# A third seven-product pair in the FFN's first product, with four smaller edits to the order of work

## The chip, the cores and the metric

The kernel runs on one core of one Trainium2 chip. The metric is the device time of one execution in microseconds (us); the time of a version is the median of its runs. TensorE (PE in the profile) multiplies, VectorE (DVE) and ScalarE (ACT) do everything elementwise, GpSimd (POOL) does almost nothing here, and SyncE (SP) issues the loads. Each engine runs its own instructions in the order in which the program lists them.

## The reference, cut to what matters

The program is a two-layer decoder trunk on 256 rows of width 2048, in float32. Each layer adds a token mixer (layer 0: pooling; layer 1: sparse attention with rotary tables), a cross attention to a memory, and a SwiGLU feed-forward block (FFN). The change is almost wholly inside the FFN:

```
FFN_HIDDEN = 5632
def swiglu(h, w_in, w_out):
    g, u = jnp.split(h @ w_in, 2, axis=-1)
    return (jax.nn.silu(g) * u) @ w_out

for i in range(2):
    ...
    x = x + swiglu(rms_norm(x, norm_ffn[i]), ffn_w_in[i], ffn_w_out[i])
```

## The kernel before

**Numbers in two halves.** Every float32 weight is split into a high part (the rounded value) and a low part (the rest), and a product is three matmuls: high times high, high times low, low times high. A weight *piece* is one load of 128 x 2048 numbers (1 MB) into one of 3 `raw` buffers. ACT makes the high part (`high`, L167) and DVE the low part (`low`, L170). Split pieces live in 8 `w` buffers of 128 x 2048.

**The FFN.** The first product is done in 11 chunks of 512 hidden columns (`chunk_in(j)`, j = 0 to 10); each needs 512 gate and 512 up columns and all 2048 input rows, that is 8 pieces or *pairs* (256 input rows each, `kp` = 0 to 7). The second product (`chunk_out`) runs after chunks 4, 8 and 10, twice each, on the hidden rows made so far. Both use `blocks`, which has four accumulators, one for each output half f (0: gate, 1: up) and each half t of the 256 rows. A *plain* pair has four *slots* of 6 matmuls, one for each accumulator; a slot is followed by `hook()`. A *seven* pair does the same 2 x 2 x 2 block product with seven products in place of eight (a Strassen form), 21 matmuls in place of 24. It needs sums of weight blocks, which DVE makes in place (L204, L207, L208), four `w` buffers (bh, bl, th, tl) in place of two, and sums of the operand (`combine`). The products that several outputs share gather in four more PSUM banks (the `sm` and `tp` ones). When the last seven pair of a chunk has ended, `mid` (L849) works these up: one ACT copy and four DVE operations.

**The end of a chunk.** The last pair is plain. After each of its slots `done(f, t)` (L864) issues a DVE addition (L867) that empties this accumulator, for f = 0 also the silu on ACT, for f = 1 a DVE multiply. The next chunk takes the four accumulator banks again. In the compiled program of the kernel before, an accumulator gets its bank at its first matmul, and takes the one that came free longest ago: the k-th slot of a new chunk waits for the k-th addition of the chunk before, whichever accumulators these are.

**What sets the order on DVE and ACT.** `hook()` (L277) runs at most one waiting job, then `split_unit()` (L227) once, or twice if the next piece is not yet split. One call issues the ACT part of the next splitting step and then the DVE part of the step *before* (`owed`): the stagger. A plain piece has two steps, a seven piece four (`d0` to `d3`). `split_seven` (L188) begins with `d0`: two lows and the 1024-wide sum L204, then `d1`: L207 and L208. A step that needs `w` buffers is only begun if no more than `cap` = 8 of them are held, by the piece in use (a seven pair gives two back after its third product, L823) and those ahead of it. So the splitting runs at most some three pieces ahead, and where it stops depends on where the seven pairs stand. `seven()` issues any job still waiting before the first seven pair of a chunk (L806).

**Other places touched.** `combine` (L415) uses `sums` buffers. `Normed.chunk` (L484) makes, beside the transposed operand, a scaled copy (`scaled`, L409) for each pair in `SEVEN`. In layer 0, `tables()` (L957) makes the rotary tables for layer 1's attention; its two functions are queued as jobs, with a delay of 6 hooks, before the last two `chunk_out` calls. The first products of the program (memory keys, pieces `xk`) stand at L609.

Of the kernel before, what the change touches and what calls it, by code (L numbers as in the profile page):

```python
# [13 lines left out]
F32R = mybir.dt.float32r  # L14
# [6 lines left out]
P = 128  # L21
# [8 lines left out]
FH = 5632  # L30
HT = FH // 512

SEVEN = (3, 5)


SEVEN_OUT = (3, 5, 11, 13, 18)
PAIRS_FIRST, SEVEN_FIRST, PAIRS = (0, 1, 2, 4, 3, 5, 6, 7), (3,), tuple(range(8))
EPS = 1e-6
TOPK = 64
KVI = 336  # L40
# [18 lines left out]
W_SHORT = 6  # L59
# [5 lines left out]
def trunk_kernel(ctx: ExitStack, tc: tile.TileContext, a: dict, out: bass.AP):  # L65
# [70 lines left out]
                for kp in range(2 * t0, 2 * t1):  # L136
                    plan(("fo", L, n, kp), a["fo"][L, n, kp], kp in SEVEN_OUT)

    state = {"load": 0, "split": 0, "cur": 0, "hook": 0, "held": 0, "cap": W_SHORT, "begun": 0}
    raws, parts, steps, owed = {}, {}, deque(), deque()  # L140
    UNIT = 1024

# [23 lines left out]
    def high(dst, src):  # L166
        A.activation(dst, src, AF.Copy)  # L167

    def low(dst, src, hi):
        V.tensor_tensor(dst, src, hi.bitcast(F32), op=ALU.subtract)  # L170
# [17 lines left out]
    def split_seven(i, t):  # L188

        r = t.rearrange("p (s c) -> p s c", s=4)  # L190
        p = {}
        own, outer = (slice(0, 1024), slice(1536, 2048)), (slice(1536, 2048), slice(0, 512))

        def a0():
            p["bh"], p["bl"] = w_tile("bh"), w_tile("bl")
            parts[i] = p
            for c in own:
                high(p["bh"][:, c], t[:, c])

        def d0():  # L200

            for c in own:
                low(p["bl"][:, c], t[:, c], p["bh"][:, c])
            V.tensor_tensor(r[:, 1:3, :], r[:, 1:4:2, :], r[:, 2:3, :].to_broadcast([P, 2, 512]), op=ALU.add)  # L204

        def d1():
            V.tensor_tensor(r[:, 3, :], r[:, 1, :], r[:, 3, :], op=ALU.add)  # L207
            V.tensor_tensor(r[:, 0, :], r[:, 3, :], r[:, 0, :], op=ALU.add)  # L208

        def a2():  # L210
            p["th"], p["tl"] = w_tile("th"), w_tile("tl")
            high(p["th"][:, 512:1536], t[:, 512:1536])

        def d2():
            low(p["tl"][:, 512:1536], t[:, 512:1536], p["th"][:, 512:1536])

        def a3():
            for c in outer:
                high(p["th"][:, c], t[:, c])

        def d3():
            for c in outer:
                low(p["tl"][:, c], t[:, c], p["th"][:, c])

        return [(2, a0, d0), (0, None, d1), (2, a2, d2), (0, a3, d3)]

    def split_unit(must=False):  # L227

        i = state["begun"]
        if not steps and i < len(pieces):  # L230
            load_to(i + 1)
            new = split_seven(i, raws[i][0]) if pieces[i][2] else split_plain(i, *raws[i])
            steps.extend((n, act, dve, i if j == len(new) - 1 else None) for j, (n, act, dve) in enumerate(new))
            state["begun"] += 1
        dve = end = None
        if steps and state["held"] + steps[0][0] <= (W_BUFS if must else state["cap"]):
            _, act, dve, end = steps.popleft()
            if act is not None:
                act()
        assert owed or dve is not None or not must  # L240
        if owed:
            fn, of = owed.popleft()
            fn()
            if of is not None:
                raws.pop(of)
                state["split"] += 1
                load_to(of + 1 + RAW_BUFS)
        if dve is not None:
            owed.append((dve, end))

    def w_get(key, ahead=0):
        i = state["cur"] + ahead
# [161 lines left out]

    def combine(f):  # L415

        s = work.tile([P, 1024], F32R, tag="sums", name="sums", bufs=4)
        c = tmp()
        a11, a21, a12, a22 = (f[:, i * P:(i + 1) * P] for i in range(4))
        s4, s2, s1, s3 = (c[:, i * P:(i + 1) * P] for i in range(4))  # L420
        V.tensor_tensor(s1, a21, a22, op=ALU.subtract)
        V.tensor_tensor(s3, a11, a21, op=ALU.subtract)
        V.tensor_tensor(s2, s1, a11, op=ALU.subtract)
        V.tensor_tensor(s4, s2, a12, op=ALU.add)
        high(s[:, 0:512], c)
        return s, lambda: low(s[:, 512:1024], c, s[:, 0:512])
# [182 lines left out]
    for j in range(4):  # L609
        wh, wl = w_get(("xk", 0, j))  # L610
        xt = ms_get(j)
        for k in range(4):
            for h in range(XH):
                mm_T(k_acc[h], wh, wl, k * 512 + h * P, xt, k, j == k == 0, j == k == 3)
            if k < 3:
                hook()
        if j == 0:
            load_x()
        if j == 2:
            load_rest()  # L620
        w_done()
        hook()

# [146 lines left out]
    def ffn(L, xn, nxt, between=()):  # L770
        hs = {}

        sums = {}
# [8 lines left out]
        def blocks(keys, operand, mid, done, t_major=0):  # L782


            acc = [acc_tile() for _ in range(4)]
            m = {}
            seven_at = [i for i in range(len(keys)) if pieces[state["cur"] + i][2]]

            def plain(i, w, f, t):
                xt, k0, _ = operand(i)  # L790
                for u in range(2):
                    ws = c(((1, 2), (0, 3))[u][f])
                    three(acc[2 * t + f], xt[:, k0 + u, t * P:(t + 1) * P], xt[:, k0 + u, S + t * P:S + (t + 1) * P],
                          w[0][:, ws], w[1][:, ws], i == 0 and u == 0, i == len(keys) - 1 and u == 1)
                if i == len(keys) - 1:
                    done(f, t, acc[2 * t + f])

            def eight(i, w):
                for f, t in ((0, 0), (0, 1), (1, 0), (1, 1)):
                    plain(i, w, f, t)  # L800
                    if (f, t) != (1, 1):
                        hook()

            def seven(i, w):
                if not m:
                    while jobs:  # L806
                        run_job()
                    m.update({1: sm_tile(), 5: sm_tile(), 6: tp_tile(), 7: tp_tile()})
                xt, k0, s = operand(i)
                first, last = i == seven_at[0], i == seven_at[-1]  # L810

                def a_(t, u):
                    return xt[:, k0 + u, t * P:(t + 1) * P], xt[:, k0 + u, S + t * P:S + (t + 1) * P]

                def s_(j):
                    return s[:, j * P:(j + 1) * P], s[:, 512 + j * P:512 + (j + 1) * P]

                bh, bl, th, tl = (w[n] for n in ("bh", "bl", "th", "tl"))
                three(acc[1], *s_(0), bh[:, c(3)], bl[:, c(3)], False, False)
                three(acc[0], *a_(0, 1), bh[:, c(0)], bl[:, c(0)], False, False)  # L820
                hook()
                three(m[1], *a_(0, 0), bh[:, c(1)], bl[:, c(1)], first, last)
                state["held"] -= W_TILES  # L823
                three(acc[2], *a_(1, 1), th[:, c(0)], tl[:, c(0)], False, False)
                hook()
                for j, (p, si) in enumerate(((5, 2), (7, 3), (6, 1))):
                    three(m[p], *s_(si), th[:, c(j + 1)], tl[:, c(j + 1)], first, last)
                    if j == 1:
                        hook()
                if last:  # L830
                    mid(m)

            n = len(keys) - t_major
            for i in range(n):
                (seven if i in seven_at else eight)(i, w_get(keys[i]))
                if i < len(keys) - 1:
                    w_done()
                    hook()
            for t in range(2 if t_major else 0):
                for i in range(n, len(keys)):  # L840
                    w = w_get(keys[i], i - n)
                    for f in range(2):
                        plain(i, w, f, t)
# [62 lines left out]
        def chunk_out(n, t0, t1, last):  # L906
# [4 lines left out]
            def mid(m):  # L911
                v, u = tmp(), tmp()
                A.activation(v, m[1], AF.Copy)
                V.tensor_tensor(u, m[6], v, op=ALU.add)
                V.tensor_tensor(xc(0, 0), xc(0, 0), v, op=ALU.add)
                for f in range(2):
                    V.tensor_tensor(xc(1, f), m[5], xc(1, f), op=ALU.add)
                    V.tensor_tensor(xc(1, f), xc(1, f), u, op=ALU.subtract)
                    if f == 0:
                        V.tensor_tensor(u, m[7], u, op=ALU.add)  # L920
                V.tensor_tensor(xc(0, 1), xc(0, 1), u, op=ALU.add)

            def operand(i):
                kp = 2 * t0 + i
# [18 lines left out]
        for gi, (t0, t1) in enumerate(GROUPS):  # L943
            last = gi == len(GROUPS) - 1
            state["cap"] = W_BUFS
            for j in range(t0 + (gi > 0), t1 + (not last)):
                chunk_in(j)
            for fn in between if last else ():
                job(fn, 6)
            for n in range(2):  # L950
                chunk_out(n, t0, t1, last)
        state["cap"] = W_SHORT
# [345 lines left out]
```

## Time and profile before

| | us |
|---|---|
| median of 3 runs (1969.64 to 1970.30) | 1970.25 |
| the profiled execution, its own time | 1970.56 |
| span of the profiled execution, first to last instruction | 1968.8 |
| PE busy | 1946.9 |
| DVE busy | 1554.8 |
| ACT busy | 1026.8 |

Times in the profile are counted from the span's start. A busy time counts overlapping instructions of an engine once. Matmuls overlap: one is listed with some 0.39 us, but they start some 0.23 us apart, and two independent DVE operations also start a little less than one duration apart.

### The profile page before, as it was taken

Reading aid. Unit: us, or ns where it says so; the run is one execution under the profiler, and the core shown is the slowest. Engines: PE = TensorE matmul, PEld = TensorE weight load, DVE = VectorE, ACT = ScalarE, POOL = GpSimd, SP = SyncE. Lnnn points to the kernel's source line nnn. Section 1 sums busy time; section 2 is a strip of 40 time slices with the busy share of each in tenths; the row PEclk is TensorE's granted clock in tenths of the full one; section 3 lists DMA queues with packets and bytes.
Section 4 is the critical chain, followed back from the end, with each engine's and each line's share of the span. In section 5 each row is a group of like instructions: output and inputs, shape, how many; then the busy total and the mean of one; then the engine's idle time right before and its main releaser. Section 6 shows DMA issues by size and latency. Waiting matters only on the chain.

```text
span 1968.8 us, 23586 instructions
## 1 busy us (share of the span) xinstructions
PE 1946.9 (99%) x8986; PEld 1617.6 (82%) x8986; DVE 1554.8 (79%) x2229; ACT 1026.8 (52%) x1462; POOL 31.6 (2%) x73
## 2 busy tenths in 40 slices
PE   9999999999999999999999999999999999999997
PEld 7888888888888888878788888888888888888886
DVE  6855888888888788887677665878887888887887
ACT  5655655554455455555445554755554455544553
POOL 0100100000000000001000000000000000000000
PEclk9999999999999999999999999999999999999999
DMA  9444545455645555544444354555545455555552
GB/s 358 173 159 164 210 174 211 174 214 190 234 173 192 192 192 214 207 158 166 172 146 171 129 189 145 200 194 209 197 171 209 175 215 195 212 191 192 192 194 106
DMA packets 53681, 372.07 MB, mean 189 GB/s; under 512 B 6336, under 2 KB 6976, under 8 KB 9536
## 3 DMA queue, kind: packets, MB, share of 16 engines
q1 hardware_dynamic: 53424, 370.52, 51.6%
q8 instruction: 70, 1.15, 0.2%
q14 instruction: 43, 0.35, 0.1%
q10 hardware_dynamic: 144, 0.05, 0.0%
HBM read 368.45 MB, written 2.10 MB: 188 GB/s over the span
## 4 chain that ended last, share of the span: by engine, by line
PE 95%; DVE 2%; ACT 1%; DMA 1%; issue 0%; SPq 0%; ACTq 0%; DVEq 0%
PE acc L776 20%; PE acc L778 20%; PE acc L777 20%; PE acc L434 5%; PE acc L432 5%; PE acc L433 5%; PE acc L457 2%; PE tp L778 1%; PE tp L777 1%; PE tp L776 1%; PE sm L777 1%; PE sm L776 1%; PE sm L778 1%; PE acc L458 1%; DMA raw<-in_xk 1%; PE tp L885 1%
## 5 line engine op out<-in xcount | busy, mean ns | idle before, releaser
L170 DVE TENSOR_TENSOR wl<-raw,wh 128x1024 fp32r<-128x1024 f32 (+2 forms) x566 | 665.4, 1210 | 110.4 <-ACT wh L167 108.8
L167 ACT ACTIVATE wh<-raw 128x1024 fp32r<-128x1024 f32 (+2 forms) x566 | 569.1, 1045 | 286.0 <-issue 106.1
L776 PE MATMUL acc<-wh,big 128*128 128x512 f32 x1616 | 634.3, 393 | 4.6 <-DVE x L930 2.8
L778 PE MATMUL acc<-wh,big 128*128 128x512 f32 x1616 | 629.9, 390 | 0.0
L777 PE MATMUL acc<-wl,big 128*128 128x512 f32 x1616 | 629.5, 390 | 0.0
L776 PEld LDWEIGHTS acc<-wh,big 128*128 128x128 f32 x1616 | 303.6, 188 | 67.2 <-DVE x L930 3.2
L778 PEld LDWEIGHTS acc<-wh,big 128*128 128x128 f32 x1616 | 303.6, 188 | 63.6
L777 PEld LDWEIGHTS acc<-wl,big 128*128 128x128 f32 x1616 | 303.9, 188 | 61.5
L432 PE MATMUL acc<-wh,big 128*128 128x512 f32 (+1 forms) x480 | 200.6, 418 | 0.0
L167 ACT ACTIVATE th<-raw 128x1024 fp32r<-128x1024 f32 x186 | 132.4, 765 | 103.4 <-DVE raw L204 99.9
L434 PE MATMUL acc<-wh,big 128*128 128x512 f32 (+1 forms) x480 | 185.9, 387 | 0.1
L433 PE MATMUL acc<-wl,big 128*128 128x512 f32 (+1 forms) x480 | 184.9, 385 | 0.0
L167 ACT ACTIVATE bh<-raw 128x1024 fp32r<-128x1024 f32 x124 | 98.0, 838 | 156.6 <-issue 93.7
L170 DVE TENSOR_TENSOR bl<-raw,bh 128x1024 fp32r<-128x1024 f32 x124 | 113.0, 953 | 84.3 <-ACT bh L167 84.3
L170 DVE TENSOR_TENSOR tl<-raw,th 128x1024 fp32r<-128x1024 f32 x186 | 151.2, 862 | 0.0
L434 PEld LDWEIGHTS acc<-wh,big 128*128 128x128 f32 x480 | 90.1, 188 | 19.1 <-DVE big L390 0.5
L433 PEld LDWEIGHTS acc<-wl,big 128*128 128x128 f32 x480 | 90.6, 189 | 16.6 <-issue 1.9
L432 PEld LDWEIGHTS acc<-wh,big 128*128 128x128 f32 x480 | 90.4, 188 | 16.3 <-issue 1.9
L457 PE MATMUL acc<-big,wh 128*128 128x512 f32 x256 | 96.2, 414 | 1.6 <-DVE big L398 1.6
L389 ACT ACTIVATE big<-tp 128x512 fp32r<-128x512 f32 x44 | 26.3, 599 | 100.1 <-PE tp L885 100.1
L204 DVE TENSOR_TENSOR raw<-raw 128x1024 f32<-128x1024 f32 x62 | 75.6, 1219 | 0.0
L458 PE MATMUL acc<-big,wl 128*128 128x256 f32 x256 | 72.7, 284 | 2.1 <-DVE wl L170 2.1
(212 smaller groups left out, 2074.4 us busy)
## 6 DMA issues: line engine op xcount, KB each, us to landing
raw<-in_fi SPq DMA_DIRECT2D x176, 1024.0 KB, 4.8
raw<-in_fo SPq DMA_DIRECT2D x88, 1024.0 KB, 4.8
raw<-in_wq SPq DMA_DIRECT2D x16, 1024.0 KB, 4.9
raw<-in_wao SPq DMA_DIRECT2D x16, 1024.0 KB, 4.9
raw<-in_xv SPq DMA_DIRECT2D x8, 1024.0 KB, 5.4
raw<-in_xq SPq DMA_DIRECT2D x8, 1024.0 KB, 4.8
raw<-in_xo SPq DMA_DIRECT2D x8, 1024.0 KB, 4.8
raw<-in_wqi SPq DMA_DIRECT2D x8, 1024.0 KB, 5.3
```

Of the source, the lines that this page charges most:

```text
L167: A.activation(dst, src, AF.Copy)
L170: V.tensor_tensor(dst, src, hi.bitcast(F32), op=ALU.subtract)
L204: V.tensor_tensor(r[:, 1:3, :], r[:, 1:4:2, :], r[:, 2:3, :].to_broadcast([P, 2, 512]), op=ALU.add)
L389: A.activation(dst_h, src, AF.Copy)
L432: T.matmul(acc[:, :w], lhsT=xh, rhs=wh[:, c0:c0 + w], start=first, stop=False)
L433: T.matmul(acc[:, :w], lhsT=xh, rhs=wl[:, c0:c0 + w], start=False, stop=False)
L434: T.matmul(acc[:, :w], lhsT=xl, rhs=wh[:, c0:c0 + w], start=False, stop=last)
L457: T.matmul(acc, lhsT=wh[:, c0:c0 + P], rhs=xt[:, k, :], start=first, stop=False)
L458: T.matmul(acc[:, S:2 * S], lhsT=wl[:, c0:c0 + P], rhs=xt[:, k, 0:S], start=False, stop=last)
L776: T.matmul(acc, lhsT=xh, rhs=wh, start=first, stop=False)
L777: T.matmul(acc, lhsT=xh, rhs=wl, start=False, stop=False)
L778: T.matmul(acc, lhsT=xl, rhs=wh, start=False, stop=last)
```

## The change

- **Seven pairs.** `SEVEN` becomes (1, 3, 5): chunks 1 to 10 of both layers have three seven pairs in place of two. Their order becomes kp = 0, 2, 1, 4, 3, 6, 5, 7, so that the seven pairs are third, fifth and seventh (before: fourth and sixth of 0 to 7). Chunk 0 keeps one seven pair, at its old place. `sums` gets a fifth buffer.
- **T2 and T4 as one.** The two outer 512-wide blocks of a seven piece are made high by one ACT and low by one DVE instruction with a stride, no longer by two each.
- **Bank order.** In the first pair of every block the two middle slots change places.
- **No stagger at first.** Until the third piece of the first product the DVE part of a step is issued with its ACT part.
- **Rotary tables.** The two jobs are queued behind `mid` of the last two `chunk_out`, one each, with a delay of 1.

```
-SEVEN = (3, 5)
+SEVEN = (1, 3, 5)
-PAIRS_FIRST, SEVEN_FIRST, PAIRS = (0, 1, 2, 4, 3, 5, 6, 7), (3,), tuple(range(8))
+PAIRS_FIRST, SEVEN_FIRST, PAIRS = (0, 1, 2, 4, 3, 5, 6, 7), (3,), (0, 2, 1, 4, 3, 6, 5, 7)
...
-        own, outer = (slice(0, 1024), slice(1536, 2048)), (slice(1536, 2048), slice(0, 512))
+        own = (slice(0, 1024), slice(1536, 2048))
+        outer = lambda v: v.rearrange("p (s c) -> p s c", s=4)[:, 0:4:3, :]
...
         def a3():
-            for c in outer:
-                high(p["th"][:, c], t[:, c])
+            high(outer(p["th"]), outer(t))
         def d3():
-            for c in outer:
-                low(p["tl"][:, c], t[:, c], p["th"][:, c])
+            low(outer(p["tl"]), outer(t), outer(p["th"]))
...
         assert owed or dve is not None or not must
+        if state["skew"]:
+            pay()
+        if dve is not None:
+            owed.append((dve, end))
+        if not state["skew"]:
+            pay()
+
+    def pay():
         if owed:
             fn, of = owed.popleft()
             fn()
...
-        if dve is not None:
-            owed.append((dve, end))
...
-        s = work.tile([P, 1024], F32R, tag="sums", name="sums", bufs=4)
+        s = work.tile([P, 1024], F32R, tag="sums", name="sums", bufs=5)
...
         if j == 2:
             load_rest()
+            state["skew"] = True
...
             def eight(i, w):
-                for f, t in ((0, 0), (0, 1), (1, 0), (1, 1)):
+                for f, t in ((0, 0), (0, 1), (1, 0), (1, 1)) if i else ((0, 0), (1, 0), (0, 1), (1, 1)):
...
                 V.tensor_tensor(xc(0, 1), xc(0, 1), u, op=ALU.add)
+                for fn in between[n:n + 1] if last else ():
+                    job(fn, 1)
...
-            for fn in between if last else ():
-                job(fn, 6)
```

## Rows read from the trace of the kernel before

**Rows 1.** Page: shares of the chain that ended last, by engine.
```profile
PE 95%; DVE 2%; ACT 1%; DMA 1%; issue 0%; SPq 0%; ACTq 0%; DVEq 0%
```
**Rows 2.** Windows (stretch, length, busy time by engine): one chunk of the first product.
```profile
core 0: us, PE busy (x) PEld busy (x) DVE busy (x) ACT busy (x) POOL busy (x), PEclk, DMA share, GB/s
286.58:329.68 43.10, 43.10 (x196) 35.71 (x195) 36.73 (x46) 23.46 (x29) 0.00 (x0) 1.00 0.54 195
```
**Rows 3.** Timeline of DVE (start, us, line, count, [idle before]), the same chunk.
```profile
299.35 1.83 DVE L170 TENSOR_TENSOR bl<-raw,bh 128x1024 fp32r<-128x1024 f32 x2 [3.00 <-ACT bh L167]
...
306.02 2.36 DVE L170 TENSOR_TENSOR wl<-raw,wh 128x1024 fp32r<-128x1024 f32 x2
...
313.57 0.69 DVE L852 TENSOR_TENSOR tmp<-tp,tmp 128x512 f32<-128x512 f32 x1 [0.21 <-ACT tmp L851]
...
316.35 3.49 DVE L170 TENSOR_TENSOR wl<-raw,wh 128x1024 fp32r<-128x1024 f32 x3
320.19 0.69 DVE L867 TENSOR_TENSOR tmp<-acc,tmp 128x512 f32<-128x512 f32 x1 [0.35 <-PE acc L778]
...
321.94 0.68 DVE L867 TENSOR_TENSOR tmp<-acc,tmp 128x512 f32<-128x512 f32 x1
...
323.77 0.68 DVE L867 TENSOR_TENSOR tmp<-acc,tmp 128x512 f32<-128x512 f32 x1
```
**Rows 4.** Timeline of PE: first matmul after the last seven pair, and of the next chunk.
```profile
313.19 0.39 PE L776 MATMUL acc<-wh,big 128*128 128x512 f32 x1
...
324.07 0.39 PE L776 MATMUL acc<-wh,big 128*128 128x512 f32 x1
```
**Rows 5.** Timeline of DVE: the four additions at the end of layer 0's chunk 10.
```profile
833.63 0.69 DVE L867 TENSOR_TENSOR tmp<-acc,tmp 128x512 f32<-128x512 f32 x1 [0.42 <-PE acc L778]
834.24 1.82 DVE L170 TENSOR_TENSOR bl<-raw,bh 128x1024 fp32r<-128x1024 f32 x2
...
837.11 0.68 DVE L867 TENSOR_TENSOR tmp<-acc,tmp 128x512 f32<-128x512 f32 x1
...
839.04 0.68 DVE L867 TENSOR_TENSOR tmp<-acc,tmp 128x512 f32<-128x512 f32 x1
...
840.49 0.68 DVE L867 TENSOR_TENSOR tmp<-acc,tmp 128x512 f32<-128x512 f32 x1
```
**Rows 6.** Timeline of PE: matmuls before which it stood idle, with the time.
```profile
15.24 0.51 PE L457 MATMUL acc<-big,wh 128*128 128x512 f32 x1 [0.75 <-DVE big L398]
16.77 0.39 PE L458 MATMUL acc<-big,wl 128*128 128x256 f32 x1 [1.03 <-DVE wl L170]
...
196.63 0.50 PE L776 MATMUL acc<-wh,big 128*128 128x512 f32 x1 [0.93 <-DVE x L525]
...
874.72 0.79 PE L776 MATMUL acc<-wh,big 128*128 128x512 f32 x1 [2.79 <-DVE x L930]
```
**Rows 7.** Windows, as in the second group, behind these stretches of idle time.
```profile
18.00:20.00 2.00, 2.00 (x7) 1.71 (x7) 0.30 (x1) 1.79 (x4) 0.00 (x0) 0.50 1.03 430
196.00:198.00 2.00, 1.37 (x6) 1.13 (x7) 1.17 (x2) 1.99 (x5) 0.00 (x0) 1.00 0.82 250
874.70:877.90 3.20, 3.18 (x9) 2.50 (x10) 3.17 (x5) 1.80 (x3) 0.00 (x0) 0.52 0.04 15
```
**Rows 8.** Timeline of DVE: the addition (layer 0, last `chunk_out` but one) that ended the longest.
```profile
873.98 0.69 DVE L930 TENSOR_TENSOR x<-acc,x 128x512 f32<-128x512 f32 x1
```
**Rows 9.** Lines by form: DVE low halves of seven pieces, of both widths.
```profile
L170 DVE TENSOR_TENSOR tl<-raw,th 128x512 fp32r<-128x512 f32 x124 | 79.8, 684 | 0.0
...
L170 DVE TENSOR_TENSOR tl<-raw,th 128x1024 fp32r<-128x1024 f32 x62 | 75.5, 1217 | 0.0
```
**Rows 10.** Timeline of ACT: a scaled operand for a seven pair, layer 0.
```profile
189.07 0.84 ACT L412 ACTIVATE tmp<-tp,gains 128x256 f32<-128x256 f32 x2 [1.65 <-DVE big L398]
```
**Rows 11.** Timeline of DVE: first and last operation of `angles`.
```profile
848.93 0.16 DVE L964 CAST posf<-pos 128x2 f32<-128x2 int32 x1
...
853.17 0.36 DVE L978 TENSOR_SCALAR tmp<-tmp 128x384 f32<-128x384 f32 x1
```

More of the change, by code (lines that the diff above doesn't have):

```diff
@@ L137, in trunk_kernel @@
                     plan(("fo", L, n, kp), a["fo"][L, n, kp], kp in SEVEN_OUT)
-    state = {"load": 0, "split": 0, "cur": 0, "hook": 0, "held": 0, "cap": W_SHORT, "begun": 0}
+    state = {"load": 0, "split": 0, "cur": 0, "hook": 0, "held": 0, "cap": W_SHORT, "begun": 0, "skew": False}
     raws, parts, steps, owed = {}, {}, deque(), deque()
```

## The prediction, as it stood before the result

> **What bounds the kernel now.** I read the page first: of the chain that ended last, 95% is PE [rows 1]. The windows of one chunk of the first product come next: PE is busy for all of its 43.10 us, DVE for 36.73, ACT for 23.46 [rows 2]. The other chunks away from the mixers look alike. So a matmul less is time gained, as long as DVE, with 6.4 us to spare in a chunk, keeps up. But the share doesn't say *when* DVE has to be done. Its one hard date is the end of the chunk: four additions must empty the accumulators before the next chunk takes their banks. So the third view is the timeline of DVE around that place [rows 3, 5], set against PE's [rows 4].
>
> **Three seven pairs: what is saved.** From the end of the last seven pair (313.19) to the next chunk (324.07) lie two plain pairs, 48 matmuls, in 10.88 us [rows 4]: 0.2267 us a matmul, 5.44 a plain pair, 1.36 a slot, 4.76 a seven pair. Each of 20 chunks loses 3 matmuls: 60 x 0.2267 = **-13.6 us**. A chunk would take 42.42 us of PE.
>
> **What it costs DVE in sum.** A seven piece takes DVE from 299.35 to 306.02, 6.67 us [rows 3]; a plain one two lows, which start 1.14 apart (three take 3.49 with the last one's tail, [rows 3]), 2.28. The exchange adds 4.39. T2 and T4 as one saves little: two of 684 ns that overlap (some 1.20 together) against one of 1217 ns (1.14 to the next start) [rows 9], some 0.06 for each of three, on ACT less still on an engine with time. DVE then needs 36.73 + 4.39 - 0.2 = 40.9 of 42.42 us: it fits, with 1.5 to spare, if it never has to wait.
>
> **Where the seven pair is put: the main term.** Before, the last seven pair is the sixth; behind it come two plain pairs, 10.88 us, in which DVE works up the shared products (313.57 to 316.35) and three lows, and still waits 0.35 us for PE before its first addition at 320.19 [rows 3]. After, the last seven pair is the *seventh*: the same work begins one pair later, and one plain pair (5.44) is left. Moreover, by the rule of 8 held buffers, when the seventh pair ends the pieces held are: last pair 2, next two plain pieces 4. Two more are allowed, so `d0` and `d1` of the next chunk's first seven piece are issued between the additions. Before, three plain pieces filled the 8 and `d0` came after the additions. The trace shows that interleaving where the next block has its seven pair in third place, at chunk 10 [rows 5]: between first and second addition stand the lows of `d0` and L204.
>
> Counted from the end E of the last seven pair, DVE does: shared products from +0.38 (313.57 - 313.19) for 2.78 [rows 3, 4], to 3.16; the one low whose turn is next, 1.14, to 4.30; then the additions at the distances of [rows 5]: second one over at 837.11 + 0.68 - 833.63 = 4.16, third at 6.09, fourth at 7.54. So the banks come free at E + 4.98, 8.46, 10.39, 11.84. PE wants them at E + 5.44 (free), 6.80, 8.16, 9.52. That a bank's release holds PE up, 0.05 us after the addition has ended, is what happened at 873.98 + 0.69, PE going on at 874.72 [rows 6, 8]. So the second slot starts at 8.51, 1.71 late; the third would at 9.87 but waits to 10.44, 0.57; the fourth 0.09. Together **2.37 us** for each change of this kind. Of 20 new chunks, 16 are followed by a block whose third pair is a seven (chunks 1, 2, 3, 5, 6, 7, 9, 10): 16 x 2.37 = **+37.9**. In the other 4 (chunks 4 and 8) a plain piece's lows stand between the additions; with the distances 2.43 and 4.26 of [rows 3] the banks come at E + 6.73 and 8.56: the third is 0.45 late, 4 x 0.45 = **+1.8**. The wait is made afresh in each chunk, since `mid` can't begin before E; behind it DVE catches up while PE stands.
>
> **The clock behind these waits.** Idle times of 0.75 and 1.03 us close together were followed by a granted clock of 0.50 (1.2 GHz), 2.79 us by 0.52 over 3.2 us, 0.93 us alone by 1.00 [rows 6, 7]. A chunk's 1.71 and 0.57, some 1.4 us apart, lie nearer to the first two. A stretch of 3.2 us at 0.52 costs 1.5 us. I take it in three of four cases: 16 x 0.75 x 1.5 = **+18**; the ends are 0 and 24.
>
> **The smaller edits.**
> - *Combine and scaled for kp 1*: ACT scales twice more (0.84, [rows 10]) in the busy stretch before each FFN, where PE already waits 0.93 at the third slot of chunk 0 [rows 6]; that instruction waits for DVE, so more than its own length may follow (0 to 1.7 each). I take 0.8 x 2 = **+1.6**. DVE's further work there has no one waiting close behind. The fifth `sums` buffer is needed since three live through the whole FFN.
> - *Bank order*: **0**. A bank goes with the place in the order, not with the accumulator; the weights of the slot that comes earlier are split by then. Were it bound to the accumulator, the third addition would free what the second slot wants: 1.3 more a chunk, 21 in all.
> - *No stagger at first*: PE waits 0.75 for an operand and 1.03 for a low half [rows 6]. The low comes a step earlier, but is then ahead of the operand's split on DVE, and that start is a queue of loads. Between -3.3 (both waits and the slow clock behind them) and +3.4 (three operands each 1.14 later): I take **-0.5**.
> - *Tables*: `angles` keeps DVE for 4.6 us [rows 11] early in the last `chunk_out` but one; at its end PE waits 2.79 [rows 6, 8]. Moved behind `mid`, it is still ahead of the same additions; `spread_tables` leaves that block. -3 to +2; I take **0**. SP's queue and POOL's are not passed by anything; a `raw` buffer comes free when its last low is done, so loads follow DVE.
>
> **Sum.** -13.6 + 37.9 + 1.8 + 18 + 1.6 - 0.5 = +45.2. On the profiled execution's 1970.56 (span 1968.8 and 1.8 around it) that is 2015.8; it stands 0.3 above the median, so **2015**.
>
> [...] Two lows of 684 ns start about 0.60 us apart, and 2 x 1.14 us is what a plain piece takes against 2 x 1.22 listed [rows 3, 9]. [...]
>
> **Rivals.**
> 1. *The additions are in time* (faster). Its place is the second bank: it decides whether DVE needs more or less than 6.80 us from E to the end of the second addition, against 8.46 above. Without `d0` between the additions (2.87 from 834.24 to 837.11, [rows 5]) it is 5.6, and there is no wait; then -13.6 + 1.6 - 0.5 stand: 1958. For it: before, `d0` comes behind the additions, and DVE's sum of 40.9 still fits. Against: the count of held buffers, and [rows 5]. [...] 9%.
> 2. *The waits are there, the clock holds*. -13.6 + 37.9 + 1.8 + 1.6 - 0.5 = +27: 1998. For it: 0.93 did nothing [rows 6, 7]. 22%.
> 3. *DVE is late inside the chunk too*: with 1.5 us to spare, a late load or a low behind ACT before `mid` moves the whole list; 0.5 a chunk more and all 16 drops of the clock (24) give -13.6 + 37.9 + 8 + 1.8 + 24 + 3.4 = +61: 2032. 14%.
> 4. *A gain cancelled by waits of some 0.85 a chunk*, about 1970: 3%.
>
> **How the numbers follow.** The forecast (waits and most drops, 2004 to 2026) has 52%; with 2 and 3 it makes 88% slower. Low end: rival 2 less the open ends of the small edits, 1990; high end: rival 3 with a little, 2036. Left out are rivals 1 and 4, 12%, and the far tails. Faster by over 0.2% (3.9 us, about what a measurement of this kernel can tell from none): 0.09; within: 0.03; slower: 0.88.
>
> **What would show it.** Right: in the waits, PE behind DVE L867, new, about 16 x 2.3 us; a chunk takes some 45 to 46.5 us between its transposes; in each, bl and L204 between the first two L867, the first of which starts 4.3 us after the last seven pair; the clock row below 1.00 in the FFN. Wrong: chunks of 42.4 us (rival 1), a wait at another place (the split of the fifth or seventh pair, a load), or a clock of 1.00 behind waits of 1.7 (rival 2). The prediction fails as a whole if `d0` isn't issued between the additions, or if a bank goes to another slot than I say.

## The result and the profile after

The changed kernel takes **2012.01 us** (median of 4 runs, 2011.57 to 2013.75) against 1969.95 (1969.07 to 1970.30) for the kernel before: ratio 1.0214, 95% interval 1.0202 to 1.0226. It is slower by 42 us, though it multiplies 60 times less. Its profiled execution took 2013.75 us, with a span of 2012.0 against 1968.8.

In the changed kernel the lines of the FFN are a few lower: the matmuls L776 to L778 are L783 to L785, `mid` is L859 to L863, the addition L867 is L875, the addition of `chunk_out` L930 is L940, and L204, L207, L208 are L206, L209, L210.

From the page of the changed kernel: busy times, the shares of the chain that ended last, the group of the matmuls that open a slot (busy, mean ns, idle time before them and its releaser).

```profile
PE 1951.6 (97%) x8926; PEld 1601.7 (80%) x8926; DVE 1638.8 (81%) x2277; ACT 1057.8 (53%) x1446; POOL 30.9 (2%) x73
...
PE 66%; DVE 19%; ACT 5%; DMA 5%; issue 4%; ACTq 0%; DVEq 0%; SPq 0%
...
L783 PE MATMUL acc<-wh,big 128*128 128x512 f32 x1456 | 578.9, 398 | 40.9 <-DVE tmp L875 30.0
```

PE's share of the chain falls from 95% [rows 1] to 66%, DVE takes 19%. The waits of PE in the changed kernel (what waited, for what, us in total, times, longest):

```profile
PE acc L783 <- DVE tmp L875: 30.0, 32, 1.8
PE acc L783 <- DVE x L940: 6.6, 10, 1.8
PE acc L783 <- DVE x L531: 3.7, 2, 1.8
PE acc L785 <- DVE sums L170: 3.0, 2, 1.7
```

The first line is new and is the one that was forecast. The windows of two chunks of layer 0, each between the same transposes of two successive chunks (columns as in [rows 2]):

```profile
336.32:381.31 44.99, 43.08 (x193) 34.90 (x191) 40.38 (x49) 24.87 (x29) 0.00 (x0) 1.00 0.53 187
381.31:424.31 43.00, 42.88 (x193) 34.91 (x192) 37.83 (x41) 23.74 (x27) 0.00 (x0) 1.00 0.59 216
```

The first one, followed by a block whose third pair is a seven, takes 44.99 us in place of 43.10 [rows 2]; the second, followed by a `chunk_out`, takes 43.00. DVE is busy for 40.38 us, near the 40.9 forecast. The granted clock is 1.00 in both. Now the timeline of DVE at the end of the first one:

```profile
368.32 0.69 DVE L860 TENSOR_TENSOR tmp<-tp,tmp 128x512 f32<-128x512 f32 x1 [0.20 <-ACT tmp L859]
...
371.11 1.21 DVE L170 TENSOR_TENSOR wl<-raw,wh 128x1024 fp32r<-128x1024 f32 x1
372.24 0.68 DVE L875 TENSOR_TENSOR tmp<-acc,tmp 128x512 f32<-128x512 f32 x1
372.84 1.81 DVE L170 TENSOR_TENSOR bl<-raw,bh 128x1024 fp32r<-128x1024 f32 x2
374.57 1.22 DVE L206 TENSOR_TENSOR raw<-raw 128x1024 f32<-128x1024 f32 x1
375.71 0.68 DVE L875 TENSOR_TENSOR tmp<-acc,tmp 128x512 f32<-128x512 f32 x1
...
377.63 0.68 DVE L875 TENSOR_TENSOR tmp<-acc,tmp 128x512 f32<-128x512 f32 x1
...
379.09 0.68 DVE L875 TENSOR_TENSOR tmp<-acc,tmp 128x512 f32<-128x512 f32 x1
```

and of PE: the first matmul after the last seven pair, and the second and third slot of the next chunk:

```profile
367.88 0.39 PE L783 MATMUL acc<-wh,big 128*128 128x512 f32 x1
...
376.54 0.47 PE L783 MATMUL acc<-wh,big 128*128 128x512 f32 x1 [1.69 <-DVE tmp L875]
...
378.37 0.50 PE L783 MATMUL acc<-wh,big 128*128 128x512 f32 x1 [0.22 <-DVE tmp L875]
```

With E, the end of the last seven pair, at 367.88 the first addition starts at E + 4.36, the second ends at E + 8.51, and the second slot starts at E + 8.66. The two lows of `d0` and the sum L206 (before: L204) stand between the first two additions.

**Where the 43.2 us of span come from.** The shift between the two traces was read at the same transposes of each chunk (243.32 became 246.53, 286.42 became 291.32, and so on). It grows by 1.69 to 2.33 us, 1.89 in the mean, at each of the 12 changes between two neighbouring chunks that can be read alone. It falls by 0.13 (0.09 to 0.17) over each of the 4 chunks that end before a `chunk_out`. It grows by 3.28 to 3.54 at the four places where two `chunk_out` and one further chunk lie between two marks, that is 1.57 more than such a chunk's 1.89. With 3.2 us up to the first mark, 4.6 between the layers and -0.6 at the end: 16 x 1.89 - 4 x 0.13 + 4 x 1.57 + 7.2 = 43.2.

### The profile page after: what moved, and what is told of

Its sections match the earlier page's. It is cut to its first block, busy times and chain, and to the rows that moved or that the text cites. A ratio compares the mean times of both kernels' runs of the same rounds, so it can differ in the third digit from the quotient of the medians.

```text
span 2012.0 us, 23516 instructions
## 1 busy us (share of the span) xinstructions
PE 1951.6 (97%) x8926; PEld 1601.7 (80%) x8926; DVE 1638.8 (81%) x2277; ACT 1057.8 (53%) x1446; POOL 30.9 (2%) x73
## 4 chain that ended last, share of the span: by engine, by line
PE 66%; DVE 19%; ACT 5%; DMA 5%; issue 4%; ACTq 0%; DVEq 0%; SPq 0%
PE acc L783 12%; PE acc L785 11%; PE acc L784 11%; PE acc L440 5%; PE acc L438 5%; PE acc L439 5%; DMA raw<-in_fi 4%; DVE bl L170 4%; ACT wh L167 3%; DVE wl L170 3%; PE acc L463 3%; DVE tl L170 2%; DVE raw L206 2%; DVE tmp L875 2%; PE acc L464 1%
## 5 line engine op out<-in xcount | busy, mean ns | idle before, releaser
L170 DVE TENSOR_TENSOR wl<-raw,wh 128x1024 fp32r<-128x1024 f32 (+2 forms) x526 | 619.6, 1209 | 101.8 <-ACT wh L167 101.0
L167 ACT ACTIVATE wh<-raw 128x1024 fp32r<-128x1024 f32 (+2 forms) x526 | 528.9, 1044 | 191.2 <-issue 57.7
L783 PE MATMUL acc<-wh,big 128*128 128x512 f32 x1456 | 578.9, 398 | 40.9 <-DVE tmp L875 30.0
L785 PE MATMUL acc<-wh,big 128*128 128x512 f32 x1456 | 569.0, 391 | 0.0
L784 PE MATMUL acc<-wl,big 128*128 128x512 f32 x1456 | 568.3, 390 | 0.0
L783 PEld LDWEIGHTS acc<-wh,big 128*128 128x128 f32 x1456 | 274.1, 188 | 119.3 <-issue 40.3
L785 PEld LDWEIGHTS acc<-wh,big 128*128 128x128 f32 x1456 | 274.0, 188 | 58.2
L167 ACT ACTIVATE th<-raw 128x1024 fp32r<-128x1024 f32 x164 | 171.4, 1057 | 188.3 <-DVE raw L206 164.9
L170 DVE TENSOR_TENSOR bl<-raw,bh 128x1024 fp32r<-128x1024 f32 (+1 forms) x164 | 149.3, 952 | 66.4 <-ACT bh L167 66.4
L170 DVE TENSOR_TENSOR tl<-raw,th 128x1024 fp32r<-128x1024 f32 x164 | 197.6, 1220 | 0.7 <-ACT th L167 0.7
L167 ACT ACTIVATE bh<-raw 128x1024 fp32r<-128x1024 f32 (+1 forms) x164 | 129.4, 837 | 128.9 <-issue 86.0
L440 PEld LDWEIGHTS acc<-wh,big 128*128 128x128 f32 x480 | 90.1, 188 | 19.1 <-DVE big L396 0.5
L438 PEld LDWEIGHTS acc<-wh,big 128*128 128x128 f32 x480 | 90.4, 188 | 16.3 <-issue 1.9
L206 DVE TENSOR_TENSOR raw<-raw 128x1024 f32<-128x1024 f32 x82 | 99.9, 1218 | 0.0
L878 ACT ACTIVATE tmp<-tmp,rs 128x512 f32<-128x512 f32 x44 | 31.9, 726 | 104.6 <-DVE tmp L875 104.4
```

The costliest lines, as they stand in the source:

```text
L438: T.matmul(acc[:, :w], lhsT=xh, rhs=wh[:, c0:c0 + w], start=first, stop=False)
L440: T.matmul(acc[:, :w], lhsT=xl, rhs=wh[:, c0:c0 + w], start=False, stop=last)
L783: T.matmul(acc, lhsT=xh, rhs=wh, start=first, stop=False)
L784: T.matmul(acc, lhsT=xh, rhs=wl, start=False, stop=False)
L785: T.matmul(acc, lhsT=xl, rhs=wh, start=False, stop=last)
```

## The experiments

The theory: PE waits for the additions at a chunk's end, because `d0` of the next block's first seven piece stands between them and `mid` starts a pair later. The rivals: DVE is simply too full, or the slow clock makes the loss, or one of the smaller edits does. Each ratio is to the kernel before on the same chip, with its 95% interval.

**Which edit costs.** The third seven pair alone, on the kernel before:

```
-SEVEN = (3, 5)
+SEVEN = (1, 3, 5)
-PAIRS_FIRST, SEVEN_FIRST, PAIRS = (0, 1, 2, 4, 3, 5, 6, 7), (3,), tuple(range(8))
+PAIRS_FIRST, SEVEN_FIRST, PAIRS = (0, 1, 2, 4, 3, 5, 6, 7), (3,), (0, 2, 1, 4, 3, 6, 5, 7)
-        s = work.tile([P, 1024], F32R, tag="sums", name="sums", bufs=4)
+        s = work.tile([P, 1024], F32R, tag="sums", name="sums", bufs=5)
```

> The kernel before with the third seven pair alone (its order and the fifth sums buffer), without the four smaller edits. Theory (the smaller edits are worth about nothing): 2009 to 2015, with the same waits of 1.7 in the second slot. Rival (the order of the slots in the first pair, or the first products, carries part of the loss): below 2000.

Measured: 2014.75 us, 1.0225 (1.0208 to 1.0242), with waits of 1.43 to 1.58 us at the second slot of the 16 changes. And the four small edits alone, with the seven pairs and their order left as before:

> The four smaller edits without the third seven pair (two as before, in their old order). Theory: 1967 to 1973, no new waits in the chunks. Rival (the order of the slots binds a bank to an accumulator): waits of about 1 us at the second slot of each block whose third pair is a seven, and 1975 or more.

Measured: 1968.81 us, 0.9993 (0.9983 to 1.0002). The changed kernel with the old order of the slots in a block's first pair:

```
-                for f, t in ((0, 0), (0, 1), (1, 0), (1, 1)) if i else ((0, 0), (1, 0), (0, 1), (1, 1)):
+                for f, t in ((0, 0), (0, 1), (1, 0), (1, 1)):
```

> The changed kernel with the slots of a block's first pair in their old order. Theory (a bank goes with the place in the order): within 1.5 us of the changed kernel, 2010.5 to 2013.5. Rival (the bank is bound to the accumulator, whose third addition frees what the second slot wants): some 21 us faster, 1991.

Measured: 2012.39 us, 1.0217 (1.0200 to 1.0235), the same as with the new order. So a bank does go with the place in the order. The loss is that of the third seven pair; the other edits together can't be told from nothing. Nor does the slow clock make it: over the whole profiled execution the granted clock is 0.996 of full speed in the kernel before and 0.995 in the changed one, a difference of some 2 us.

**Without `d0` between the additions.** The changed kernel, but the next block's seven piece isn't begun until the last pair of a block has ended:

```
-        if steps and state["held"] + steps[0][0] <= (W_BUFS if must else state["cap"]):
+        still = state["quiet"] and not must and len(steps) == 4
+        if steps and not still and state["held"] + steps[0][0] <= (W_BUFS if must else state["cap"]):
...
                     w_done()
+                    state["quiet"] = i == len(keys) - 2 and not t_major
                     hook()
+            state["quiet"] = False
...
```

> The changed kernel, but a seven piece of the next block is not begun from the hook ahead of a block's last pair until that pair has ended; so no step of it stands between the four additions. Theory (the additions come too late because d0 stands between them): second addition over at E + 5.6 instead of 8.5, before the bank is wanted at 6.80, so the waits behind L875 go and the saving shows: 1958 to 1964. Rival (DVE as a whole, 40.9 of 42.4 us a chunk, is too full for three seven pairs): the wait moves to another place and the time stays above 1990.

Measured: 1977.12 us, 1.0035 (1.0022 to 1.0048): 34.9 of the 42 us are gone with the same work on every engine. The waits behind the additions fall from 30.0 us in 32 places to 7.9 in 10. So DVE isn't too full; its order was at fault. But 1958 to 1964 was missed. At all of the 10 places ACT waits 1.43 to 2.73 us for a load shortly before, and `mid` starts at E + 1.23 to 2.62; at the other chunk ends such a wait is 0.71 at the most, and `mid` starts at E + 0.27 to 0.50. One of the 10 shows how. ACT, then DVE, then PE of this version, with E = 364.89:

```profile
364.05 2.01 ACT L167 ACTIVATE wh<-raw 128x1024 fp32r<-128x1024 f32 x2 [1.89 <-DMA raw<-in_fi]
```
```profile
365.14 1.22 DVE L170 TENSOR_TENSOR wl<-raw,wh 128x1024 fp32r<-128x1024 f32 x1 [1.53 <-ACT wh L167]
366.57 0.69 DVE L863 TENSOR_TENSOR tmp<-tp,tmp 128x512 f32<-128x512 f32 x1 [0.21 <-ACT tmp L862]
...
370.49 1.88 DVE L878 TENSOR_TENSOR tmp<-acc,tmp 128x512 f32<-128x512 f32 x3
```
```profile
364.89 0.39 PE L784 MATMUL acc<-wh,big 128*128 128x512 f32 x1
...
371.32 0.47 PE L784 MATMUL acc<-wh,big 128*128 128x512 f32 x1 [0.83 <-DVE tmp L878]
```

A load lands late, ACT's two highs start 1.89 us late, the copy for `mid` is behind them on ACT and the low ahead of it on DVE. So `mid` starts at E + 1.68, not E + 0.44 as above, and the first addition at E + 5.60.

**`mid` a pair earlier.** The changed kernel with the seven pairs third, fifth and sixth, two plain pairs behind the last:

```
-... PAIRS = ... (0, 2, 1, 4, 3, 6, 5, 7)
+... PAIRS = ... (0, 2, 1, 4, 3, 5, 6, 7)
```

> The changed kernel with the pairs of a chunk in the order 0, 2, 1, 4, 3, 5, 6, 7: still three seven pairs and the same work for each engine, but the last is the sixth, with two plain pairs behind it. Theory (it is the place of the last seven pair, 5.44 us later, that makes the additions late): the shared products are worked up before the last pair, the second addition is over just before its bank is wanted, waits of at most 0.3 a chunk: 1958 to 1970. Rival (DVE too full): two seven pairs in a row need 13.3 us of DVE in 10 us of PE and a wait for tl appears at the sixth pair; above 1990.

Measured: 1996.97 us, 1.0133 (1.0118 to 1.0148). A miss. The number is in the rival's range, but the rival's sign, a wait for `tl`, doesn't appear in PE's waits. ACT, DVE and PE at such a chunk's end, with E = 360.62:

```profile
360.24 2.01 ACT L167 ACTIVATE wh<-raw 128x1024 fp32r<-128x1024 f32 x2 [2.25 <-DMA raw<-in_fi]
```
```profile
361.33 1.23 DVE L170 TENSOR_TENSOR wl<-raw,wh 128x1024 fp32r<-128x1024 f32 x1 [1.33 <-ACT wh L167]
362.76 0.69 DVE L860 TENSOR_TENSOR tmp<-tp,tmp 128x512 f32<-128x512 f32 x1 [0.21 <-ACT tmp L859]
...
368.95 0.68 DVE L875 TENSOR_TENSOR tmp<-acc,tmp 128x512 f32<-128x512 f32 x1
369.55 1.81 DVE L170 TENSOR_TENSOR bl<-raw,bh 128x1024 fp32r<-128x1024 f32 x2
371.29 1.21 DVE L206 TENSOR_TENSOR raw<-raw 128x1024 f32<-128x1024 f32 x1
372.43 0.68 DVE L875 TENSOR_TENSOR tmp<-acc,tmp 128x512 f32<-128x512 f32 x1
```
```profile
360.62 0.39 PE L783 MATMUL acc<-wh,big 128*128 128x512 f32 x1
...
372.63 0.39 PE L785 MATMUL acc<-wh,big 128*128 128x512 f32 x1
373.25 0.47 PE L783 MATMUL acc<-wh,big 128*128 128x512 f32 x1 [0.23 <-DVE tmp L875]
```

Here the second addition ends at 373.11, and PE wanted its bank at 372.86 (0.23 behind the matmul before). But a late load has put `mid` at E + 2.14 and the first addition at E + 8.33. `d0` between the additions doesn't make the second one late by itself: at chunk 10 of the kernel before it stands there too, also with two plain pairs behind the last seven pair, and PE doesn't wait. The DVE line there is the start of `mid`, the PE lines are E and the next block's second slot:

```profile
826.94 0.69 DVE L852 TENSOR_TENSOR tmp<-tp,tmp 128x512 f32<-128x512 f32 x1 [0.20 <-ACT tmp L851]
```
```profile
826.63 0.39 PE L776 MATMUL acc<-wh,big 128*128 128x512 f32 x1
...
838.87 0.39 PE L776 MATMUL acc<-wh,big 128*128 128x512 f32 x1
```

There `mid` begins at E + 0.31 and the first addition at E + 7.00. The second is over at E + 11.16 [rows 5], and PE takes the bank at E + 12.24. In the version with `mid` a pair earlier, `mid` starts at E + 2.14 to 4.64 at all 16 changes, at 15 of them behind a wait of ACT for a load (2.25 to 3.56 us). So it isn't a clean test of the place of `mid`; it shows again that loads land late (ACT waits 42.6 us for those of the first product, against 14.7 in the changed kernel).

The listed wait of 0.23 costs more than 0.23. The two matmuls start 0.62 apart, 0.39 more than usual, and the one after follows at 373.56, 0.31 later. So a wait that reads 0.2 costs some 0.4 to 0.5 us. I had counted waits by their listed length.

**What is one low worth?** The changed kernel with one low of 1.14 us made twice in `d0` of the first seven piece of chunks 1 to 10; what it adds writes the same numbers again:

```
+        key = pieces[i][0]
+        first = key[0] == "fi" and key[2] > 0 and key[3] == 1
...
             for c in own:
                 low(p["bl"][:, c], t[:, c], p["bh"][:, c])
+            if first:
+                low(p["bl"][:, 0:1024], t[:, 0:1024], p["bh"][:, 0:1024])
```

> The changed kernel with one more 1024-wide low half (a repeat, 1.14 us of DVE) in d0 of the first seven piece of chunks 1 to 10, so between the first and the second addition of the block before. Theory (the second bank is what PE waits for): the wait grows by 1.14 in the 14 changes from chunk to chunk and by as much in the 4 from the second product to the first, 2 x 0.8 behind chunk 0: +22 us, 2034, if the granted clock stays 1.00; 2056 if each of the 14 longer waits (2.9 us) is followed by 1.6 us lost to a low clock. Rival (another step ends last): less than 5 us more.

Measured: 2051.68 us, 1.0411 (1.0394 to 1.0429), 39.7 us more, and 36.8 us of span in the two profiled executions. Between the transposes, 10 of the chunk changes with the extra low can be read alone. The 2 with no low clock behind them grew by 1.09 and 1.24 us: that is the low, in full on PE's path. The 8 with a low clock grew by 1.83 to 2.51 us, 2.22 in the mean. The 2 changes from chunk 10 to a `chunk_out`, which the edit doesn't touch, grew by -0.09 and 0.03. So some 22 us (18 x 1.14 + 2 x 0.8, as forecast) are the low itself. The rest is the clock: between the begin of layer 0's FFN and the last chunk it falls at 15 places, in the changed kernel at 2. Two of these waits and the granted clock behind them (PE's timeline, then windows of 4 us):

```profile
336.15 0.47 PE L787 MATMUL acc<-wh,big 128*128 128x512 f32 x1 [2.98 <-DVE tmp L879]
...
382.24 0.77 PE L787 MATMUL acc<-wh,big 128*128 128x512 f32 x1 [2.82 <-DVE tmp L879]
```
```profile
336.15:340.15 4.00, 3.78 (x15) 2.69 (x16) 3.75 (x6) 2.51 (x3) 0.00 (x0) 1.00 0.00 0
382.24:386.24 4.00, 4.00 (x11) 3.22 (x12) 3.76 (x6) 2.50 (x3) 0.00 (x0) 0.59 0.02 4
```

Of the 14 waits of 2.79 to 3.08 us behind additions at chunk ends, 10 were followed by a low clock and 4 weren't. A stretch as the second costs 4 x 0.41 = 1.6 us of the clock, but net such a change lost only some 1.1 us more (2.22 against 1.09 and 1.24), since the shorter wait at its third slot is then gone. In the changed kernel none of the 16 waits of 1.52 to 1.85 us at chunk ends was.

**Both remedies.** The late begin and `mid` a pair earlier:

> The late beginning of the next seven piece and the order with the last seven pair in sixth place, together. Theory (in the first alone a late load ahead of the shared products moved DVE's list by 1 to 1.7 us; with one more plain pair behind them that is covered): no waits behind L875 but single ones, chunks of 42.4 to 42.6: 1959 to 1966. Rival (DVE's sum is too full as such): 1975 or more, as with the late beginning alone.

Measured: 1972.39 us, 1.0009 (1.0000 to 1.0019). A miss again: 4.7 better than the late begin alone, but 6 to 13 us above the forecast. Its chunks without a wait take 42.42 us, so the matmuls' saving is there in these. What is left are the waits at the ends of the FFN (3.6 us for the operand, 3.4 for the sums of the first seven pair, 2.4 behind the last `chunk_out` but one), 4.0 us for an operand at the program's start, 3.0 in 6 places behind additions at chunk ends, and late loads: ACT waits 42.0 us for first-product loads, against 14.7 in the changed kernel.

**Without the cost where the FFN begins.** The same with kp 3, 5, 7 for seven pairs, so that kp 1 needs no scaled operand, the sums of chunk 0's seven pair finished first, and the old stagger:

```
-SEVEN = (1, 3, 5)
+SEVEN = (3, 5, 7)
-... PAIRS = ... (0, 2, 1, 4, 3, 5, 6, 7)
+... PAIRS = ... (0, 1, 3, 2, 5, 7, 4, 6)
-    state = {... "skew": False, ...}
+    state = {... "skew": True, ...}
-                        late.append(then)
+                        late.insert(0 if kt0 // 2 in SEVEN_FIRST else len(late), then)
```

> As the one before (late beginning, last seven pair sixth), and without three small costs of the change: the seven pairs are kp 3, 5 and 7, so no scaled copy is made in the busy stretch ahead of the FFN; the sums of chunk 0's seven pair are finished first; the first products are staggered as before. Theory: the waits behind L531 fall from 1.83 to 0.93, those behind the sums go (2 x 1.5), with the slow clock behind one of them 1.7: some 5 to 7 us less than the one before, 1953 to 1960. Rival (they are hidden by something that ends as late): within 2 us of the one before.

Measured: 1966.56 us, 0.9983 (0.9974 to 0.9992): 5.8 us less, as large as forecast for this step, from a start that was 12 us too high. That the step's size came out is in part luck. Read at the transposes of the two profiled executions (6.6 us of span), the two begins of the FFN gave 6.6 us, but the low clock that was to go there hadn't been there in the version before. The program's start gave 2.2 and the end of layer 0's FFN 1.3, which weren't forecast, and the chunks lost 3.2. It is a little faster than the kernel before. PE still waits 5.2 us in 9 places behind additions, and ACT 48.6 us for first-product loads.

**Are late loads the rest?** The same, each first-product load in two transfers of 1024 columns:

```
-            nc.sync.dma_start(t[:, :w], pieces[i][1])
+            for c in range(0, w, 1024 if pieces[i][0][0] == "fi" else w):
+                e = min(w, c + (1024 if pieces[i][0][0] == "fi" else w))
+                nc.sync.dma_start(t[:, c:e], pieces[i][1][:, c:e])
```

> The version of the run before this one (third, fifth and sixth pair seven, the next block's seven piece begun late, no cost at the mixers: 1966.6 us), with one edit: each load of a first-product piece (1 MB) is made as two transfers of 1024 columns, so that the first `high` can begin when half has landed and half a `raw` buffer can be loaded again as soon as its own low is done. Theory: what keeps that version above the 1957 us of its matmuls are loads that land late (ACT waits 48.6 us in 29 places for a first-product load, up to 3.7 us). Then those waits fall by half or more, and the time by 3 to 8 us, to 1959 to 1964. Rival A: the loads are late because a transfer begins late (its buffer is held till the last low) and a half begins hardly earlier, or half loads take longer in sum: ACT's waits stay within a quarter of 48.6 us and the time at 1965 to 1968. Rival B: the loads aren't what holds PE up; the waits fall, but the time stays at 1965 to 1968, and PE's waits behind additions keep their 5 us.

Measured: 1959.69 us, 0.9947 (0.9934 to 0.9961): 6.9 us less. ACT's waits for these loads before (first line) and with the halves (second line), then PE's waits behind additions before and with the halves:

```profile
ACT wh L167 <- DMA raw<-in_fi: 48.6, 29, 3.7
```
```profile
ACT wh L169 <- DMA raw<-in_fi: 34.0, 42, 2.6
```
```profile
PE acc L784 <- DVE tmp L878: 5.2, 9, 1.4
```
```profile
PE acc L786 <- DVE tmp L880: 2.1, 2, 1.8
```

The time is in the theory's range; the waits fell by less than half, but the longest went from 3.7 to 2.6 us, and 5.5 of the 6.3 us between the two spans were gained in the chunks. Now whole chunks run without a wait (windows of two, as above):

```profile
287.07:329.49 42.42, 42.42 (x192) 35.13 (x191) 40.74 (x49) 24.73 (x30) 0.00 (x0) 1.00 0.58 198
329.49:371.91 42.42, 42.42 (x192) 35.14 (x191) 40.45 (x49) 24.55 (x30) 0.00 (x0) 1.00 0.58 199
```

DVE does its 40.5 to 40.7 us of work inside 42.42 us of PE. To see whether the halves are a gain of their own, the kernel before with the same edit:

> The kernel before (two seven pairs) with the one edit of the run before: first-product loads as two transfers of 1024 columns. It asks whether the halves are a gain of their own or only pay for the third seven pair. Theory: in the kernel before PE is busy for the whole of a chunk (43.10 of 43.10 us) and no wait of its chunks is behind a load, so the halves have nothing to give: 1968 to 1972. Rival: loads cost the kernel before something too (its ACT waits 17.9 us for them); then 1962 to 1967, and most of what the halves brought isn't owed to the third seven pair.

Measured: 1968.52 us, 0.9994 (0.9985 to 1.0003): no difference that can be told. With two seven pairs the halves bring 3 us at the most; with three they carry the gain. Last, the second product's loads as halves too:

> The version with half loads in the first product (1959.7 us), with the second product's loads made as halves too. There ACT still waits 36.2 us in 25 places for a second-product load. Theory: in the second product PE has no wait in its waits view but at its ends, so ACT's waits there fall by half and the time stays at 1958 to 1961. Rival: these late loads delay the next chunk's first pieces; then 1954 to 1958.

Measured: 1957.58 us, 0.9939 (0.9926 to 0.9951), 12.9 us less than the kernel before. That it is so near to the 13.6 that the matmuls saved are worth is in part chance: by the transposes the chunks are 9.8 us shorter, so 3.8 are still lost there, and 2.6 come from the last `chunk_out` but one of layer 0, where a wait of 2.79 us with a low clock behind it became one of 1.61 without. ACT's waits for second-product loads fall from 36.2 to 22.2 us. It lies just below the theory's range, in the rival's, and its 2 us to the version before it are too few to say where they come from. A fourth `raw` buffer, the plainest cure for late loads, wasn't tried.

## Why the prediction was right, and where it was not

The sign, the place and the size came out: 2015 forecast, 2012.01 measured. The mechanism, the waits for PSUM banks behind `d0` and a later `mid`, was the forecast's. That the number came within 3 us is luck: the clock's term was 18 too high, and short and missing terms nearly cancelled it.

- **Matmuls saved, -13.6**: right. A chunk without waits takes 42.42 us, the figure forecast.
- **DVE's sum, 40.9 a chunk**: right (40.4 to 40.8).
- **The waits at 16 chunk changes, +37.9**: the ledger held. First addition at E + 4.36 for 4.30, second bank at 8.51 for 8.46, second slot at 8.66 for 8.51; the bank order was as read. The slot came 0.15 after the addition's end, not 0.05. The shift of 1.89 a chunk and the 0.68 saved make 2.57 a change in place of 2.37, together 41.1; the 0.2 more is this later start and the slow restart behind each wait, which I hadn't counted. That the cause is `d0` among the additions is shown: with `d0` begun later the loss is nearly gone, and one low more in `d0` adds its own length. That the later `mid` is needed for it too is shown by chunk 10 of the kernel before, where `d0` stands between the additions and PE doesn't wait. That `d0` is begun there because of the count of held buffers was read from the code and agrees with every order seen; no run changes the count by itself.
- **Chunks 4 and 8, +1.8**: 4 x (0.68 - 0.13) = 2.2. Right.
- **The clock, +18: wrong, close to 0 in its place.** I likened a pair of idle times of 1.71 and 0.57 to the starts of 0.75 and 1.03 [rows 6, 7]; the 0.93 that did nothing turned out to be the better likeness. No chunk change was followed by a low clock; the one new fall in the FFN, behind 1273.68, is in the 7.2 below. Rival 2 was right about the clock, and gave 1998 since the next terms were missing.
- **Missed: the change from a second `chunk_out` to the next chunk, 4 x 1.57 = +6.3.** The prediction has no term for it. That block's `mid` has eight operations on DVE, not four, so the first addition is late even with two plain pairs behind it, and `d0` stands behind it too. With `d0` begun later no wait is left at these four places. DVE in the changed kernel (start of `mid`, its last operation, three lows and the first addition), then PE at the next chunk's second slot:

```profile
493.56 0.69 DVE L922 TENSOR_TENSOR tmp<-tp,tmp 128x512 f32<-128x512 f32 x1 [0.20 <-ACT tmp L921]
...
498.15 0.68 DVE L929 TENSOR_TENSOR x<-x,tmp 128x512 f32<-128x512 f32 x1
498.75 3.49 DVE L170 TENSOR_TENSOR wl<-raw,wh 128x1024 fp32r<-128x1024 f32 x3
502.16 0.68 DVE L940 TENSOR_TENSOR x<-acc,x 128x512 f32<-128x512 f32 x1
```
```profile
506.46 0.47 PE L783 MATMUL acc<-wh,big 128*128 128x512 f32 x1 [0.81 <-DVE x L940]
```

- **The mixers' end and the FFN's begin, +1.6 and -0.5: too small.** Together with the two ends of the program it is 7.2. PE waits 1.83 us for the operand where it waited 0.93 [rows 6], as forecast in each layer. Unforeseen was that chunk 0's seven pair then waits for its sums (two cases, 3.0 us in the waits above), since with kp 1 three combinations instead of two are queued ahead of their low halves. And one of the two waits of 1.83 us drew the clock down:

```profile
197.79 0.50 PE L783 MATMUL acc<-wh,big 128*128 128x512 f32 x1 [1.83 <-DVE x L531]
...
1273.68 0.50 PE L783 MATMUL acc<-wh,big 128*128 128x512 f32 x1 [1.83 <-DVE x L531]
```
```profile
197.79:201.79 4.00, 4.00 (x17) 3.30 (x18) 2.73 (x3) 4.00 (x7) 0.00 (x0) 1.00 0.58 238
1273.68:1277.68 4.00, 4.00 (x12) 3.15 (x13) 2.73 (x3) 4.00 (x7) 0.00 (x0) 0.63 0.96 385
```

- **Tables, 0**: 0.56 + 1.84 us of waits (at 892.28 and 895.75) in place of 2.79, with a low clock behind them as before (0.57 over 4 us from 895.75). Right. **Bank order, 0, and no stagger**: nothing measurable.

So the working's own sum with the measured terms is -13.6 + 41.1 + 2.2 + 6.3 + 7.2 = 43.2, against -13.6 + 37.9 + 1.8 + 18 + 1.6 - 0.5 = 45.2: the clock was 18 too high, the other terms 16 too low.

**The rules weighed.** The first addition, the two lows and L206 behind it, listed with 0.68, 1.81 and 1.22 us, take 375.71 - 372.24 = 3.47 us from start to start, as in [rows 5] (3.48), so they overlap here too. The Trainium skill, "VectorE: DVE Perf Modes", section "The DRAIN you can't avoid", lets an operation wait until the pipe of the one before has emptied, but adds that one that isn't held back starts earlier; the trace agrees with the latter. The Trainium skill, "Perfetto Trace Analysis", section "Identifying the Most-Contended Engine", would optimize the engine with the highest occupancy first, and judges TensorE by its FLOPs and by the busy share of its weight loads in place of the matmuls' (97% against DVE's 81% in the changed kernel). In the chunk of [rows 2] the weight loads are busy for 35.71 us and DVE for 36.73, nearly level. The runs show that no such share settles it: three seven pairs a chunk lost 42 us or gained 13, depending mainly on when DVE's work came, because a share doesn't show a date.

## What to carry to other kernels

An engine with time to spare on average can still be late at each handover. Before giving it more work, make a ledger from the handover's start to the time at which each buffer is wanted back, with everything that the program's order puts between. When such a change loses, move the work out from between before giving it up: here three seven pairs a chunk went from 42 us slower to 13 us faster with no matmul less, by when the next piece is begun, which pairs they are and where they stand, the order of the sums, the old stagger and the size of the loads. Removing one wait shows the next (additions, then sums and operand, then loads), so the full gain comes only with the last of them.

## What the runs showed of the hardware

- The clock can't be told from the length of one wait. Behind waits of 1.52 to 1.85 us at 16 chunk changes of the changed kernel it held. The wait for the operand at the FFN's begin was 1.81 to 1.85 us long in 14 cases (two each in the changed kernel and six other versions): 6 were followed by a low clock (0.61 to 0.69 over 4 us) and 8 by 1.00, and in two of the seven one case went each way. Of 14 waits of 2.79 to 3.08 us, 10 were followed by a drop. What decides between equal waits stays open.
- A wait listed with 0.2 us for a PSUM bank takes 0.4 to 0.5 us from PE: the matmul starts some 0.15 us after the addition's end, and the next one 0.31 in place of 0.23 us behind it.
- A load in two halves of 512 KB lands hardly sooner each by the page (4.7 us in the median from issue to landing, against 4.8 for 1 MB in the version before), yet the version with halves was 6.9 us faster. The edit lets the work on the first half begin, and its part of the buffer be refilled, earlier; which of the two brings the gain isn't shown.
